# Four small edits in a two-layer transformer trunk: operand places for the first matmuls, and the order and pieces of the last stage

## The chip, the cores and the metric

The kernel runs on one core of one Trainium2 chip. The metric is the device time of one execution in microseconds (us); the times shown are the median of three runs. One execution was also recorded by the hardware profiler, and its trace is what all row times below come from. Five engines work side by side, each through its own list of instructions in order: TensorE (PE, with the weight loads as a row PEld), VectorE (DVE), ScalarE (ACT), GpSimd (POOL) and SyncE (SP), which here issues the large transfers. SBUF is the memory on the chip that the engines read and write; PSUM is the memory that receives the matmul results.

## The reference

Two decoder layers over 512 tokens of width 1024, float32. Cut to what the change touches:

```python
def reference(x, p, positions, ...):
    cos, sin = _rope_tables(positions)
    for i in range(2):
        h = _rms_norm(x, mix_norm[i])
        if i == 0: x = x + _attn_conv_mixer(h, cos, sin, hy_w_in[0], ...)   # q, k, v, cb, cc, cx = split(h @ w_in)
        else:      x = x + _gla_mixer(h, gla_w_in[0], ...)
        x = x + _conv_ffn(_rms_norm(x, ffn_norm[i]), ...)
        x = x + _per_layer_embedding(x, p[i], ple_norm[i], ple_w_gate[i], ple_w_proj[i])
    return x

def _per_layer_embedding(x, p_i, norm, w_gate, w_proj):
    gate = jax.nn.sigmoid(_rms_norm(x, norm) @ w_gate)      # (512 x 1024) @ (1024 x 1024)
    return gate * (p_i @ w_proj)                            # (512 x 256) @ (256 x 1024)
```

The change touches the first matmuls of layer 0 (keys and values, `h @ w_in[:, 512:768]`) and the last stage of layer 1, the per-layer embedding that ends the program.

## The kernel before, in words

**Precision.** A float32 product is made of three matmuls in the type fp32r. Each operand is split into a high part (an ACT copy that rounds) and a low part (a DVE subtraction of the high part from the operand); then high x high, high x low and low x high are summed in PSUM. `mm3` (L162 to L164) does this for most products, `add` in the last stage (L1369 to L1371) for its blocks. So every weight block costs one ACT copy and one DVE subtraction before TensorE may use it.

**Places of split weights.** `wide(tag, at)` gives a tile of 128 partitions by 1088 elements, of which 1024 are used from element `at` on. There are two tags, `wh` for high and `wl` for low parts, with three tiles each, reused in turn. `cut` (L126) is the usual splitter of weights and uses `at` = 0 for both; `cut_blocks` (L811), used in the feed-forward stages (matmuls L872 to L874), uses 16 for `wh` and 48 for `wl`, that is 64 and 192 bytes.

**The start.** In `mixer0`, the input is loaded in four column groups, turned by TensorE (L469), scaled and split, and at once multiplied with the key and value columns of `w_in` (256 columns). Here the activations are the stationary operand of the matmul and the split weights, from `weight(c)`, are the moving one: 8 features of 128 rows, 4 token tiles and 3 matmuls, 96 matmuls of 256 columns in all. The first 12 are at L457 to L460, the rest come through `mm3`. The order on PE, DVE and ACT is the written one here (`manual_schedule`). The query matmuls (512 columns) follow.

**The last stage.** `ple1` (L1323) computes the gate product with a block scheme of Strassen's kind: seven block products instead of eight, with the names `e1`, `s1`, `s2`, `s3`, `s4`, `o2`, `o1` for the activation forms, in this order. Their weights are blocks of 512 x 512: the plain ones `b11`, `b22`, `b21` and differences of them, made in place by `minus` (L1358, two DVE instructions of 128x1024 each, called halves below). `chunk` (L1341) splits half a block: one ACT copy (L1348) and one DVE subtraction (L1349) of 128x1024; its results go to `wh`/`wl` tiles or to tiles called `four`, by a counter, three and three in turn. The products accumulate in four PSUM banks, `X[0]`, `X[1]`, `Q[0]`, `Q[1]`; ACT copies some of the partial sums out (`ka`, `kd`, `kb`; `kd` is made by `keep`, L1401) and DVE adds them later (`summed`, L1407). `back` turns 128 tokens of the residual `x` to token order (TensorE L1377, ACT copy L1381). `proj` multiplies the per-layer input with a half of `w_proj` that `chunk` has split (`wj`): per token tile six matmuls of 512 columns, L162 to L164, into a PSUM bank `pa`. `finish` ends an output tile: ACT sigmoid (L1413), DVE product with the projection (L1414), DVE sum with `x` (L1415), and a transfer to DRAM issued by SP (L1416). All of PE, DVE and ACT follow the written order in this part.

Around the first edit the written order is: `load_p` (the split of the per-layer input, L109/L110), product `s1`, `minus(b12, b22, b12)` (both halves), `kd = keep(Q)`, `wt3 = chunks(b12)` (two splits), `wj = chunk(...)`, four steps of `s2`, two `back`, the other four steps of `s2`, the copies `kb` of `X`, two `proj`, the splits `w22` of `b22`, `minus(b11, b21, b11)`, the first split `wt4[0]`, then product `s3` with `wt3`. A "step" is one j and one i: three matmuls of 512 columns.

At the very end the last product `o1` is done for token tile 0 (512 columns, `Y[0]`) and then for token tile 1 in three pieces of columns: 256 into half of `Q[1]`, then 128 and 128 into two parts of `X[0]`; each piece is finished by itself while the next is multiplied.

Of the kernel before, what the change touches and what calls it, by code (L numbers as in the profile page):

```python
# [56 lines left out]
class Kernel:  # L57
# [65 lines left out]
        t = self.wp.tile([P, 2048], F32, tag="raw", name=self.nm("raw"), bufs=2)  # L123
        return t[:, : na * nb].rearrange("p (a b) -> p a b", b=nb)

    def cut(self, rv, by):  # L126

        nc = self.nc
        na, nb = rv.shape[1:]
        parts = []  # L130
        n = 2 if na * nb > 1024 else 1
        for k in range(n):
            if by == "b":
                a, b = na, nb // n
                v = rv[:, :, k * b : (k + 1) * b]
            else:
                a, b = na // n, nb
                v = rv[:, k * a : (k + 1) * a, :]
            h, l = self.wide("wh"), self.wide("wl")
            hv = h[:, : a * b].rearrange("p (a b) -> p a b", b=b)  # L140
            lv = l[:, : a * b].rearrange("p (a b) -> p a b", b=b)
            nc.scalar.activation(hv, v, AF.Copy)  # L142
            nc.vector.tensor_tensor(lv, v, hv.bitcast(F32), ALU.subtract)  # L143
            parts.append((hv, lv))

        def get(i, c0, c1):
            if by == "b":
                b = nb // n
                k = c0 // b
                h, l = parts[k]  # L150
                return h[:, i, c0 - k * b : c1 - k * b], l[:, i, c0 - k * b : c1 - k * b]
            a = na // n
            h, l = parts[i // a]
            return h[:, i % a, c0:c1], l[:, i % a, c0:c1]

        return get
# [265 lines left out]
    def mixer0(self):  # L422
        nc, a, tc = self.nc, self.a, self.tc
        with tc.tile_pool(name="m0", bufs=1) as mp:
# [3 lines left out]
            kvr = self.raw(ND, 256)  # L428
# [14 lines left out]
            wkv = []  # L443
# [28 lines left out]
                return pss  # L472

            def weight(c):
                wkv.append(self.cut(kvr[:, 2 * c : 2 * c + 2, :], "a"))

            def operand(m, ps):
                hl = self.pair(self.fp, "a0", "a1")
# [38 lines left out]
            h = HD // 2  # L517
# [339 lines left out]
    def seven(self, od, ws, xg, forms, keep=True):  # L857
# [6 lines left out]
        W, V = self.pa(), self.pa()[:, :H]  # L864
        X, Y = self.ps(), self.ps()
        plain, t13, t2 = ws

        def product(out, w, c, x, first=False):
            kw = dict(skip_group_check=True)
            for j in range(ND // 2):  # L870
                (wh, wl), (xh, xl) = w(j, c), x(j)
                mm(out, wh, xh, start=first and j == 0, stop=False, **kw)  # L872
                mm(out, wh, xl, start=False, stop=False, **kw)  # L873
                mm(out, wl, xh, start=False, stop=j == ND // 2 - 1, **kw)  # L874

        def tokens(u, half):
            c = slice(half * H, (half + 1) * H)
            return lambda j: (xg[2 * j + u][0][:, c], xg[2 * j + u][1][:, c])
# [4 lines left out]
        nc.scalar.copy(X[:, left], W[:, left])  # L883
        nc.scalar.copy(Y[:, left], W[:, left])
        yield
# [5 lines left out]
        product(X[:, left], plain, 1, tokens(1, 0))  # L891
        product(Y[:, left], t2, 0, s2)
        nc.scalar.copy(X[:, right], Y[:, left])  # L893
        yield
        last = self.cut_blocks(od)
        product(X[:, right], t13, 1, s3)
        nc.scalar.copy(Y[:, right], X[:, right])
        yield
        product(Y[:, left], last, 1, s4)
        product(X[:, right], last, 0, tokens(1, 1))  # L900
# [422 lines left out]
    def ple1(self, fp):  # L1323
# [3 lines left out]
        nc, a, tc = self.nc, self.a, self.tc  # L1327
# [4 lines left out]
        H, J = D // 2, ND // 2  # L1332

        def block(u, c, own):
            raw = self.raw(J, H) if own else self.four(fp, F32)
            nc.sync.dma_start(raw, wg[u, :, :, c * H : (c + 1) * H])
            return raw
# [3 lines left out]
        def chunk(src):  # L1341
            if count[0] % 6 < 3:
                h, l = (self.wide(g).rearrange("p (a b) -> p a b", b=H) for g in ("wh", "wl"))
            else:
                four = self.four(fp)
                h, l = four[:, :2], four[:, 2:]
            count[0] += 1
            nc.scalar.activation(h, src, AF.Copy)  # L1348
            nc.vector.tensor_tensor(l, src, h.bitcast(F32), ALU.subtract)  # L1349
            return h, l  # L1350

        def chunks(raw):
            return [chunk(raw[:, 2 * q : 2 * q + 2, :]) for q in range(2)]

        def minus(out, x, y):
            for q in range(2):
                c = slice(2 * q, 2 * q + 2)
                nc.vector.tensor_tensor(out[:, c, :], x[:, c, :], y[:, c, :], ALU.subtract)  # L1358

# [28 lines left out]
        def proj(t, w):  # L1388
            pj = self.pa()
            for k in range(2):  # L1390
                self.mm3(pj, sl(pT[k], t), (w[0][:, k, :], w[1][:, k, :]), start=k == 0, stop=k == 1)
            return pj
# [27 lines left out]
        b12 = block(0, 1, True)  # L1420
        pin = self.p_halves(1)
        b22 = block(1, 1, False)
        wj_raw = self.four(fp, F32)
# [6 lines left out]
        X, Q = [[self.ps() for _ in range(2)] for _ in range(2)]  # L1430
        both = (0, H)
        with tc.manual_schedule(engines={ET.PE, ET.DVE, ET.Activation}):
            add(X, "e1", w11, first=True)
            wt1.append(chunk(b11[:, 2:, :]))
            minus(b11, b22, b11)
            steps = [(j, i, both, Q[i]) for j in range(J) for i in range(2)]
            add(None, "s1", wt1, first=True, order=steps[:2])

            self.end_norm()
            ka = [self.sp.tile([P, S], F32, tag="acc", name=self.nm("keep"), bufs=1), self.sq()]  # L1440
            for k, x in zip(ka, X):
                nc.scalar.copy(k, x)
            wt2 = chunks(b11)
            pT = self.load_p(1, fp, pin)
            add(None, "s1", wt1, order=steps[2:])
            minus(b12, b22, b12)
            kd = keep(Q, "R")
            wt3 = chunks(b12)
            wj = chunk(wj_raw[:, 2:, :])
            steps = [(j, i, both, X[i]) for j in range(J) for i in range(2)]  # L1450
            add(None, "s2", wt2, order=steps[:4])
            xs = [back(1, t) for t in (2, 3)]
            add(None, "s2", wt2, order=steps[4:])
            kb = [self.sq(), result()]
            for k, x in zip(kb, X):
                nc.scalar.copy(k, x)
            pjs = [proj(t, wj) for t in (2, 3)]
            w22 = chunks(b22)
            minus(b11, b21, b11)
            wt4 = [chunk(b11[:, :2, :])]  # L1460
            nc.scalar.activation(self.few(NT, "rlo"), self.r, AF.Sigmoid)
            add(X, "s3", wt3)
            ss = [summed(X[t], kd[t]) for t in (0, 1)]
            for t in (0, 1):
                finish(1, t + 2, ss[t], xs[t], pjs[t], ss[t])
            steps = [(j, i, both, Q[i]) for j in range(J) for i in range(2)]
            add(None, "s4", w22, order=steps[:6])
            xs = [back(1, t) for t in (0, 1)]
            pjs = [proj(t, wj) for t in (0, 1)]
            wt4.append(chunk(b11[:, 2:, :]))  # L1470
            wj = chunk(wj_raw[:, :2, :])
            add(None, "s4", w22, order=steps[6:])
            ss = [summed(Q[t], kb[t]) for t in (0, 1)]

            halves = ((0, H // 2), (H // 2, 3 * H // 4), (3 * H // 4, H))
            Y = [Q[0], Q[1][:, : H // 2], X[0][:, : H // 4], X[0][:, H // 4 : H // 2]]
            for t in (0, 1):
                finish(1, t, ss[t], xs[t], pjs[t], ss[t])
            nc.scalar.copy(Y[0], ka[0])
            nc.scalar.copy(Y[1], ka[1][:, : H // 2])  # L1480
            steps = [(j, i, both, X[i]) for j in range(J) for i in range(2)]
            add(None, "o2", wt4, order=steps[:6])
            xs = [back(0, t) for t in (2, 3)]
            pjs = [proj(t, wj) for t in (2, 3)]
            w21 = chunks(b21)
            add(None, "o2", wt4, order=steps[6:])
            for t in (0, 1):
                finish(0, t + 2, X[t], xs[t], pjs[t])
                if t == 0:
                    nc.scalar.copy(X[0][:, : H // 2], ka[1][:, H // 2 :])  # L1490
            add(None, "o1", w21, order=[(j, 0, both, Y[0]) for j in range(J)])
            xs = [back(0, t) for t in (0, 1)]
            pjs = [proj(t, wj) for t in (0, 1)]
            finish(0, 0, Y[0], xs[0], pjs[0])
            for y, c in zip(Y[1:], halves):
                add(None, "o1", w21, order=[(j, 1, c, y) for j in range(J)])
                finish(0, 1, y, xs[1], pjs[1], None, *c)
# [471 lines left out]
```

## Time and profile before

| | us |
|---|---|
| median of 3 runs | 1209.83 (1209.56 to 1209.96) |
| the profiled execution's own time | 1209.6 |
| its span on the core | 1207.8 |
| PE busy in the span | 1199.9 |
| DVE busy | 968.9 |
| ACT busy | 665.2 |

The views used are: the page (busy time and the chain of work that ended last), the table of waits of one engine, the timeline of one engine (start in us, duration in us, engine, line, operation, output from inputs, shape, count; in brackets the idle time before it and what ended it) and the list of transfers. Rows of the timeline that follow each other with the same line, tiles and shape are merged, with their count at the end. Matmuls are pipelined: the duration of one (0.39 us at 512 columns) is longer than the distance from its start to the next start (0.23 us), so lengths of PE work are read from starts.

### The profile page before, as it was taken

Reading aid. Unit: us, or ns where it says so; the run is one execution under the profiler, and the core shown is the slowest. Engines: PE = TensorE matmul, PEld = TensorE weight load, DVE = VectorE, ACT = ScalarE, POOL = GpSimd, SP = SyncE. Lnnn points to the kernel's source line nnn. Section 1 sums busy time; section 2 is a strip of 40 time slices with the busy share of each in tenths; the row PEclk is TensorE's granted clock in tenths of the full one; section 3 lists DMA queues with packets and bytes.
Section 4 is the critical chain, followed back from the end, with each engine's and each line's share of the span. In section 5 each row is a group of like instructions: output and inputs, shape, how many; then the busy total and the mean of one; then the engine's idle time right before and its main releaser. Section 6 shows DMA issues by size and latency. Waiting matters only on the chain.

```text
span 1207.8 us, 17724 instructions
## 1 busy us (share of the span) xinstructions
PE 1199.9 (99%) x7025; PEld 1038.0 (86%) x7025; DVE 968.9 (80%) x1529; ACT 665.2 (55%) x1082; POOL 43.8 (4%) x64
## 2 busy tenths in 40 slices
PE   9999999999999999999999999999999999999998
PEld 8877788999898888888988988889998899888877
DVE  6886687899998987746679876678999898978595
ACT  7466455656555644534563555555565555645364
POOL 2600000000000000000100000000000000000000
PEclk9999999999999999999999999999999999999999
DMA  7321322423233333232322222322242423323501
GB/s 221 95 83 47 95 71 70 140 70 115 96 107 103 102 126 96 96 104 79 113 93 70 72 69 71 105 74 102 73 138 70 140 70 132 122 88 107 199 1 70
DMA packets 111271, 117.61 MB, mean 97 GB/s; under 512 B 2856, under 2 KB 106466, under 8 KB 111188
## 3 DMA queue, kind: packets, MB, share of 16 engines
q1 hardware_dynamic: 109824, 115.35, 29.3%
q8 instruction: 55, 0.90, 0.3%
q0 software_dynamic: 560, 0.42, 0.3%
q10 hardware_dynamic: 804, 0.70, 0.2%
q14 instruction: 28, 0.23, 0.1%
HBM read 114.37 MB, written 2.10 MB: 96 GB/s over the span
## 4 chain that ended last, share of the span: by engine, by line
PE 85%; DVE 9%; ACT 2%; issue 1%; DMA 1%; POOL 1%; ACTq 0%; DVEq 0%; POOLq 0%
PE ps L162 12%; PE ps L163 12%; PE ps L164 12%; PE pa L163 6%; PE pa L162 6%; PE pa L164 6%; PE ps L872 5%; PE ps L874 5%; PE ps L873 5%; PE pa L872 2%; PE pa L874 2%; PE pa L873 2%; DVE wl L143 2%; PE ps L1369 1%; PE ps L1371 1%
## 5 line engine op out<-in xcount | busy, mean ns | idle before, releaser
L142 ACT ACTIVATE wh<-raw 128x1024 fp32r<-128x1024 f32 (+4 forms) x154 | 152.4, 991 | 153.8 <-PE ps L163 109.4
L143 DVE TENSOR_TENSOR wl<-raw,wh 128x1024 fp32r<-128x1024 f32 (+4 forms) x154 | 175.8, 1142 | 49.6 <-ACT wh L142 49.1
L819 ACT ACTIVATE wh<-raw 128x1024 fp32r<-128x1024 f32 x78 | 82.8, 1062 | 119.0 <-DVE raw L844 65.6
L932 DVE SCALAR_TENSOR_TENSOR zt<-z,vfa,zt 128x510 f32<-128x510 f32 (+1 forms) x176 | 130.8, 745 | 11.7 <-ACT zt L930 11.2
L820 DVE TENSOR_TENSOR wl<-raw,wh 128x1024 fp32r<-128x1024 f32 x78 | 95.3, 1222 | 20.9 <-ACT wh L819 20.9
L930 ACT ACTIVATE zt<-z,vfb 128x512 f32<-128x512 f32 x88 | 71.0, 809 | 29.0 <-DVE four L983 12.8
L162 PE MATMUL ps<-b,wh 128*128 128x512 f32 x192 | 76.8, 400 | 0.0
L163 PE MATMUL ps<-b,wh 128*128 128x512 f32 x192 | 75.1, 391 | 0.0
L164 PE MATMUL ps<-b,wl 128*128 128x512 f32 x192 | 75.0, 391 | 0.0
L163 PE MATMUL pa<-b,wh 128*128 128x512 f32 x176 | 69.0, 392 | 0.0
L163 PE MATMUL pa<-a,wh 128*128 128x512 f32 x176 | 69.0, 392 | 0.0
L162 PE MATMUL pa<-a,wh 128*128 128x512 f32 x176 | 69.0, 392 | 0.0
L162 PE MATMUL pa<-b,wh 128*128 128x512 f32 x176 | 69.0, 392 | 0.0
L164 PE MATMUL pa<-a,wl 128*128 128x512 f32 x176 | 68.4, 389 | 0.0
L164 PE MATMUL pa<-b,wl 128*128 128x512 f32 x176 | 68.4, 389 | 0.0
L872 PE MATMUL ps<-four,wh 128*128 128x256 f32 x232 | 65.1, 281 | 0.5 <-ACT ps L893 0.5
L874 PE MATMUL ps<-four,wl 128*128 128x256 f32 x232 | 64.4, 277 | 0.0
L873 PE MATMUL ps<-four,wh 128*128 128x256 f32 x232 | 64.2, 277 | 0.0
L162 PE MATMUL ps<-a,wh 128*128 128x512 f32 x160 | 63.0, 394 | 0.0
L163 PE MATMUL ps<-a,wh 128*128 128x512 f32 x160 | 62.6, 392 | 0.0
L164 PE MATMUL ps<-a,wl 128*128 128x512 f32 x160 | 62.5, 391 | 0.0
L162 PE MATMUL ps<-uh,wh 128*128 128x512 f32 x128 | 50.3, 393 | 0.0
(475 smaller groups left out, 3498.5 us busy)
## 6 DMA issues: line engine op xcount, KB each, us to landing
raw<-in_ffn_w_up_dram SPq DMA_DIRECT2D x44, 1024.0 KB, 5.0
raw<-in_ffn_w_down_dram SPq DMA_DIRECT2D x13, 1024.0 KB, 4.7
raw<-in_hy_w_in_dram SPq DMA_DIRECT2D x8, 1024.0 KB, 5.2
raw<-in_gla_w_in_dram SPq DMA_DIRECT2D x8, 1024.0 KB, 5.3
raw<-in_ffn_w_down_dram SPq DMA_DIRECT2D x8, 768.0 KB, 4.1
raw<-in_ple_w_gate_dram SPq DMA_DIRECT2D x6, 1024.0 KB, 4.8
raw<-in_hy_w_out_dram SPq DMA_DIRECT2D x16, 256.0 KB, 3.9
raw<-in_gla_w_out_dram SPq DMA_DIRECT2D x4, 1024.0 KB, 4.7
```

The costliest lines, as they stand in the source:

```text
L142: nc.scalar.activation(hv, v, AF.Copy)
L143: nc.vector.tensor_tensor(lv, v, hv.bitcast(F32), ALU.subtract)
L162: mm(out, lh, rh, start=start, stop=False, **kw)
L163: mm(out, lh, rl, start=False, stop=False, **kw)
L164: mm(out, ll, rh, start=False, stop=stop, **kw)
L819: nc.scalar.activation(h, src, AF.Copy)
L820: nc.vector.tensor_tensor(l, src, h.bitcast(F32), ALU.subtract)
L872: mm(out, wh, xh, start=first and j == 0, stop=False, **kw)
L873: mm(out, wh, xl, start=False, stop=False, **kw)
L874: mm(out, wl, xh, start=False, stop=j == ND // 2 - 1, **kw)
L930: nc.scalar.activation(y, z, AF.Identity, scale=w2[:, f : f + 1], bias=bb[:, f : f + 1])
L932: nc.vector.scalar_tensor_tensor(out=y[:, tap:], in0=z[:, : S - tap], scalar=w[:, f : f + 1], in1=y[:, tap:], op0=ALU.mult, op1=ALU.add,)
```

## The change

1. **Places of the key and value weights.** `cut` takes a pair `at`; `weight(c)` in `mixer0` passes (48, 16), so the high parts of the key and value weights start 192 bytes and the low parts 64 bytes into their tiles. Every other caller keeps 0.
2. **The projection's split first.** `wj = chunk(wj_raw[:, 2:, :])` moves ahead of `kd = keep(Q, "R")` and of the splits of `b12`.
3. **The second half of a difference later.** `minus(b12, b22, b12)` is done in two calls: the first half where it was, the second half after the split of the first half, `wt3[0]`. The split of the second half, `wt3[1]`, moves from there to behind the copies `kb` of the sums `X` (on ACT, behind them in order; on DVE it stays the next subtraction after the second half).
4. **The last 512 columns in two pieces.** `halves` has two entries, 256 and 256 columns; the second piece goes into half of `X[0]`.

With the edits 2 and 3 the tiles of the splits change too: the counter hands the projection the place in turn that the first half of `b12` had, and so on by one; all are of the kind `wh`/`wl` as before. On DVE the order in the stage is now: difference half one, `wj`, `wt3[0]`, difference half two, `wt3[1]`, `w22`. On ACT: `wj`, the two copies `kd`, `wt3[0]`, the two `back` copies, the two copies `kb`, `wt3[1]`, `w22`. With edit 4, PE has 12 matmuls fewer, DVE two instructions, ACT and SP one each. No instruction changes its place on POOL, and no other transfer moves.

```diff
-    def cut(self, rv, by):
+    def cut(self, rv, by, at=(0, 0)):
...
-            h, l = self.wide("wh"), self.wide("wl")
+            h, l = self.wide("wh", at[0]), self.wide("wl", at[1])
...
-                wkv.append(self.cut(kvr[:, 2 * c : 2 * c + 2, :], "a"))
+                wkv.append(self.cut(kvr[:, 2 * c : 2 * c + 2, :], "a", (48, 16)))
...
-        def minus(out, x, y):
-            for q in range(2):
+        def minus(out, x, y, parts=(0, 1)):
+            for q in parts:
...
-            minus(b12, b22, b12)
+            minus(b12, b22, b12, (0,))
+            wj = chunk(wj_raw[:, 2:, :])
             kd = keep(Q, "R")
-            wt3 = chunks(b12)
-            wj = chunk(wj_raw[:, 2:, :])
+            wt3 = [chunk(b12[:, :2, :])]
+            minus(b12, b22, b12, (1,))
...
             pjs = [proj(t, wj) for t in (2, 3)]
+            wt3.append(chunk(b12[:, 2:, :]))
             w22 = chunks(b22)
...
-            halves = ((0, H // 2), (H // 2, 3 * H // 4), (3 * H // 4, H))
-            Y = [Q[0], Q[1][:, : H // 2], X[0][:, : H // 4], X[0][:, H // 4 : H // 2]]
+            halves = ((0, H // 2), (H // 2, H))
+            Y = [Q[0], Q[1][:, : H // 2], X[0][:, : H // 2]]
```

## The prediction

> **What bounds the kernel.** I read the page first, then the waits of PE, then the timelines of the first 22 us and the last 60 us.
>
> ```profile
> span 1207.8 us, 17724 instructions
> PE 1199.9 (99%) x7025; PEld 1038.0 (86%) x7025; DVE 968.9 (80%) x1529; ACT 665.2 (55%) x1082; POOL 43.8 (4%) x64
> ```
>
> ```profile
> PE pa L163 <- DVE wl L1349: 0.9, 1, 0.9
> PE pa L653 <- ACT pT L661: 0.5, 1, 0.5
> PE ps L1369 <- ACT so L1413: 0.5, 1, 0.5
> ```
>
> PE is busy 1199.9 of 1207.8 us: matmul work sets the time. Three of its waits stand above (total, times, longest). The first is a projection matmul in the last stage that waits for the low part of its weights, the third is the last 128-column piece. So time can be gained only by shortening PE's work, its few waits, or the tail after its last matmul. The edits aim at one of each kind.
>
> **The change part by part.**
>
> *Edits 2 and 3, the wait of the projection.* PE, then DVE and ACT of the stage:
>
> ```profile
> 1164.87 0.39 PE L1371 MATMUL ps<-four,a 128*128 128x512 f32 x1
> 1165.29 0.50 PE L162 MATMUL pa<-wh,four 128*128 128x512 f32 x1
> 1166.74 0.50 PE L163 MATMUL pa<-wl,four 128*128 128x512 f32 x1 [0.95 <-DVE wl L1349]
> 1167.08 0.39 PE L164 MATMUL pa<-wh,four 128*128 128x512 f32 x1
> ...
> 1172.09 0.39 PE L1369 MATMUL ps<-wh,a 128*128 128x512 f32 x1
> ...
> 1179.69 0.48 PE L162 MATMUL pa<-wh,four 128*128 128x512 f32 x1
> ...
> 1180.23 0.39 PE L164 MATMUL pa<-wh,four 128*128 128x512 f32 x1
> ```
>
> ```profile
> 1159.65 1.28 DVE L110 TENSOR_TENSOR four<-pa,four 128x512 fp32r<-128x512 f32 x2
> 1160.85 2.35 DVE L1358 TENSOR_TENSOR raw<-four,raw 128x1024 f32<-128x1024 f32 x2
> 1163.18 2.37 DVE L1349 TENSOR_TENSOR wl<-raw,wh 128x1024 fp32r<-128x1024 f32 x2
> 1165.47 1.22 DVE L1349 TENSOR_TENSOR wl<-four,wh 128x1024 fp32r<-128x1024 f32 x1
> 1168.16 2.36 DVE L1349 TENSOR_TENSOR four<-four,four 128x1024 fp32r<-128x1024 f32 x2 [1.48 <-ACT four L1348]
> ...
> 1174.33 1.37 DVE L1407 TENSOR_TENSOR so<-ps,keep 128x512 f32<-128x512 f32 x2 [0.26 <-PE ps L1371]
> ```
>
> ```profile
> 1158.61 1.08 ACT L1401 COPY keep<-ps 128x512 f32<-128x512 f32 x2
> 1162.09 2.20 ACT L1348 ACTIVATE wh<-raw 128x1024 fp32r<-128x1024 f32 x2 [2.40 <-DVE raw L1358]
> 1164.20 1.04 ACT L1348 ACTIVATE wh<-four 128x1024 fp32r<-128x1024 f32 x1
> 1165.14 1.05 ACT L1381 COPY zt<-pa 128x512 f32<-128x512 f32 x2
> 1166.08 0.60 ACT L1456 COPY sq<-ps 128x512 f32<-128x512 f32 x1
> ```
>
> From the projection's first to its third matmul PE takes 1167.08 - 1165.29 = 1.79 us here and 1180.23 - 1179.69 = 0.54 us in the next projection, which does not wait: the stall costs 1.25 us (the bracket says 0.95; the rest is the restart). Its cause is order: DVE makes two difference halves and two other low parts first and reaches `wl<-four` only at 1165.47.
>
> With the new order DVE does, from 1160.85 on and one every 1.15 us (2.35 for two): difference half one, the projection's low part (1162.0 to 1163.2), the low part of `wt3[0]` (1163.2), half two (1164.3 to 1165.5). The projection's operand is there 2.1 us before PE asks for it at 1165.29; its ACT copy goes in at 1158.61, in front of the `kd` copies. These come 1 us later, and nothing is behind them: their first reader is the sum at 1174.33, and `wt3[0]`'s copy needs difference half one, so it stays at 1162.1. So 1.25 us go; the lower bound is the bracket's 0.95.
>
> What is late next? `wt3[1]`. Its ACT copy is now behind the copies of `X`, which wait for the last matmul of `s2` (1164.87 + 0.39 = 1165.3): with 0.5 us for that copy it starts at 1165.8 and ends at 1166.9, the DVE part (1.23) at 1168.1. PE wants it in the third quarter of `s3`, at 1172.09 now and 1.25 earlier then: 1170.84, so 2.7 us are left. `w22` follows on DVE at 1168.1, as before (1168.16), and the difference of `b11` behind it and the sums at 1174.33 stay where they are or come 0.5 us earlier; no queue gets longer. I add nothing for a new wait; the range keeps up to 0.3 us for one.
>
> The moved steps issue no transfers. One more place: the turn of the `wh`/`wl` tiles has moved by one, so the second half of `wt4` might get the tile that the two later projections still read. By the rows they end then at 1181.4 (1.25 before 1182.7); copy and subtraction (1.06 + 1.23) would make it ready at 1183.8, and PE asks for it at 1185.3 (1186.59 now):
>
> ```profile
> 1182.28 0.39 PE L164 MATMUL pa<-wh,four 128*128 128x512 f32 x1
> ...
> 1186.59 0.39 PE L1369 MATMUL ps<-wh,a 128*128 128x512 f32 x1
> ```
>
> Even then 1.5 us are left.
>
> *Edit 4, the last pieces.*
>
> ```profile
> 1199.29 0.28 PE L1369 MATMUL ps<-wh,b 128*128 128x256 f32 x1
> ...
> 1200.72 0.22 PE L1369 MATMUL ps<-wh,b 128*128 128x128 f32 x1
> ...
> 1202.68 0.33 PE L1369 MATMUL ps<-wh,b 128*128 128x128 f32 x1 [0.51 <-ACT so L1413]
> ```
>
> ```profile
> 1202.33 0.33 SPq L1416 DMA_DIRECT2D out_dram<-so  x1
> ```
>
> ```profile
> 1205.31 0.33 SPq L1416 DMA_DIRECT2D out_dram<-so  x1
> ```
>
> ```profile
> out_dram<-so SPq DMA_DIRECT2D x1, 128.0 KB, 1.8
> out_dram<-so SPq DMA_DIRECT2D x2, 64.0 KB, 1.5
> ```
>
> The 256-column piece takes 1200.72 - 1199.29 = 1.43 us for its 12 matmuls; the 128-column piece behind it takes 1202.68 - 1200.72 = 1.96 us until its successor may start, because that one, in the same bank, waits for the sigmoid that reads it. From its first matmul to the issue of its transfer the 256-column piece takes 1202.33 - 1199.29 = 3.04 us. The new last piece is the same work, starts at 1200.72, and so issues at 1203.76 instead of 1205.31: 1.55 us. ACT and DVE are clear of the piece before it: that one is done at its issue, 1202.33, and the new piece's last matmul starts only at 1200.72 + 11 x 0.12 = 1202.04, its sigmoid after its end. The larger transfer lands in 1.8 instead of 1.5 us: the net is 1.25 us. Bounds: 1.0 and 1.55.
>
> *Edit 1, the places.* Two steady runs of 256-column matmuls, first and last rows: 41 distances of the key/value matmuls, 23 in the feed-forward.
>
> ```profile
> 16.21 0.28 PE L162 MATMUL pa<-wh,a 128*128 128x256 f32 x1
> ...
> 21.13 0.28 PE L164 MATMUL pa<-wh,a 128*128 128x256 f32 x1
> ```
>
> ```profile
> 189.57 0.28 PE L872 MATMUL ps<-a,wh 128*128 128x256 f32 x1
> ...
> 192.17 0.28 PE L874 MATMUL ps<-four,sq 128*128 128x256 f32 x1
> ```
>
> That is 4.92 / 41 = 0.120 us against 2.60 / 23 = 0.113 us for the same shape. The faster run has its stationary operands 64 and 192 bytes into their tiles, the slower has everything at 0. Edit 1 makes the same distances between moving and stationary operand, with the roles exchanged. If the distance is what matters, 96 matmuls gain 0.007 us each, at most 0.65 us. The first 12 are written in another order, and transposes interrupt the start three times, so I take 0.5. The other end: no row shows a steady run above 0.120, so a loss isn't seen; I allow the half of the gain, 0.3 us, since roles and not only distances may count. ACT and DVE splits cost the same at either place (128x1024: 1058 and 1062 ns on ACT, in the rows of L142 and L819).
>
> ```profile
> L142 ACT ACTIVATE wh<-raw 128x1024 fp32r<-128x1024 f32 x119 | 125.6, 1058 | 116.4 <-PE ps L163 80.3 <-PE ps L873 16.8 <-PE ps L164 7.6
> L819 ACT ACTIVATE wh<-raw 128x1024 fp32r<-128x1024 f32 x78 | 82.8, 1062 | 119.0 <-DVE raw L844 65.6 <-PE ps L873 16.3 <-PE ps L163 14.2
> ```
>
> Does a gain at 20 us reach the end? PE waits at 88 us for `pT` (0.5 us, above), the end of a long ACT and DVE chain. That chain starts when PE hands over the first query:
>
> ```profile
> 41.56 0.69 ACT L570 ACTIVATE q<-ps,rtok 128x512 f32<-128x512 f32 x1 [2.34 <-PE ps L164]
> ```
>
> So it moves with PE, and no later wait of PE names a transfer. I let all of it through.
>
> The Trainium skill, TensorE: Matmul & The Clock Gate, "Step-by-step: what each phase is for", speaks against this edit: the weight load and the moving operand have separate read ports, and loading the next weights "doesn't steal SBUF read bandwidth from the running matmul". By that rule edit 1 gives 0 and the sum is 2.5 us; by the two rows above, 3.0. The rows differ in pitch with the same clock and shape, so I go by them, but they differ in roles too, and the rule keeps a chance below.
>
> *Sum.* 1.25 + 1.25 + 0.5 = 3.0 us. The profiled execution of 1209.6 becomes 1206.6; the median shown is 0.2 above it, so I predict 1206.8.
>
> **The rivals.**
>
> *The places do nothing* (the 0.120 comes from the roles of the operands or from what precedes, not from the distance). For it: the 512-column runs have their operands at 0 too, and no pair of rows in this trace differs in place alone. Time 1209.8 - 2.5 = 1207.3. This is the rival that the quoted rule stands behind; it is just at the limit of what counts as a difference.
>
> *Part of the last stage's gain returns as a new wait*, or the key/value matmuls get slower by the 0.3 us allowed. Against it stand 2.7 and 1.5 us of slack. Time about 1208.0.
>
> *Slower: the third quarter of `s3` becomes the wait.* Place: PE at L1370 with `wt3[1]`, whose copy now stands behind the copies of `X` on ACT. Price: every us past 1170.84 is a us of PE time. If it were ready at 1173.3 the 2.5 us of the stage would be gone; for a slowdown of 0.2% it must come 2.4 us later still or more, about 1176, that is 8 us after my 1168.1, for instance if the ACT copy waited for `s3`'s first half or for the sums. Time then 1212. Nothing before it in the queue waits that long in the rows.
>
> **How the numbers follow.** A measurement here tells about 0.2%, 2.4 us, from no change: the limit is 1207.4. Chances: forecast 0.62 (1206.2 to 1207.3), places do nothing 0.20, partial return 0.13, slower 0.05. The forecast is faster nearly always (0.59); the second rival, at 1207.3, a little more often than not (0.12); the third stays within 0.2%. So 0.71 faster, 0.24 same, 0.05 slower. Range: the best ends, 1.25 + 1.55 + 0.65 = 3.45, give 1206.4, with 0.2 for the scatter of the runs 1206.2; at the top, 0.95 + 1.0 and nothing from edit 1 give 1207.9.
>
> **What would show it.** Edit 1: distances of 0.113 to 0.115 in the key/value run, and the first query matmul 0.5 us earlier than 21.49; at 0.120 it failed. Edits 2 and 3: the wait of L163 for L1349 gone from PE's list, `s3`'s third quarter without a bracket. Edit 4: two 256-column runs of 1.43 us each, no bracket between them, 3.0 us from the last run's first matmul to the last issue. The forecast is wrong if a new wait of PE over 0.5 us appears between 1165 and 1196, or if the start's gain is taken back by a longer wait at 88 us.
>
> ```profile
> 21.49 0.50 PE L162 MATMUL ps<-wh,a 128*128 128x512 f32 x1
> ```

## The result, and the profile after

The changed kernel takes 1206.60 us, the median of nine runs (1206.16 to 1207.34), against 1209.87 us for the kernel before on the same chip (nine runs, 1209.14 to 1210.16). The ratio is 0.9975 with a 95% interval of 0.9966 to 0.9983: 3.3 us faster, a quarter of a percent, and the interval leaves "no change" outside. 1206.8 was predicted. The profiled execution took 1206.43 us, of it 1204.7 in the span.

Page of the changed kernel: the span, and the busy time of each engine.

```profile
span 1204.7 us, 17692 instructions
PE 1197.7 (99%) x7013; PEld 1036.9 (86%) x7013; DVE 968.3 (80%) x1527; ACT 665.3 (55%) x1081; POOL 43.8 (4%) x64
```

The span is 3.1 us shorter and PE's busy time 2.2 us (1199.9 to 1197.7). Its waits (total, times, longest, in us), as far as the list goes:

```profile
PE pa L198 <- DVE mhalf L186: 1.3, 1, 1.3
PE ps L872 <- ACT ps L893: 0.5, 2, 0.3
PE pa L653 <- ACT pT L661: 0.5, 1, 0.5
PE ps L162 <- DVE kT L1558: 0.2, 1, 0.2
```

The two waits of the last stage, L163 for `wl` and L1369 for `so`, are gone and no new wait of that stage has come in. Timeline of PE after, in the last stage and in the key/value run (start, duration):

```profile
1161.15 1.04 PE L1377 MATMUL pa<-cf,xT 128*128 128x128 f32 x8
...
1164.53 0.39 PE L1371 MATMUL ps<-four,a 128*128 128x512 f32 x1
1164.76 0.39 PE L162 MATMUL pa<-wh,four 128*128 128x512 f32 x1
1164.99 0.39 PE L163 MATMUL pa<-wl,four 128*128 128x512 f32 x1
1165.21 0.39 PE L164 MATMUL pa<-wh,four 128*128 128x512 f32 x1
...
1197.39 0.28 PE L1369 MATMUL ps<-wh,b 128*128 128x256 f32 x1
...
1198.83 0.28 PE L1369 MATMUL ps<-wh,b 128*128 128x256 f32 x1
...
1200.15 0.28 PE L1371 MATMUL ps<-four,a 128*128 128x256 f32 x1
```

```profile
16.26 0.28 PE L162 MATMUL pa<-wh,a 128*128 128x256 f32 x1
...
21.08 0.28 PE L164 MATMUL pa<-wh,a 128*128 128x256 f32 x1
21.45 0.50 PE L162 MATMUL ps<-wh,a 128*128 128x512 f32 x1
```

The projection now runs at 0.23 us per matmul from the last matmul of `s2` on, without a gap. The last two pieces start 1198.83 - 1197.39 = 1.44 us apart, with no bracket (a bracket at the end of a row is the idle time before it). The key/value run, however, takes 4.82 / 41 = 0.1176 us per matmul: hardly less than the 0.120 before, and far from the 0.113 that was predicted for it.

DVE and ACT after, in the same stage, show the new order:

```profile
1160.50 1.21 DVE L1358 TENSOR_TENSOR raw<-four,raw 128x1024 f32<-128x1024 f32 x1
1161.63 1.21 DVE L1349 TENSOR_TENSOR wl<-four,wh 128x1024 fp32r<-128x1024 f32 x1
1162.84 1.23 DVE L1349 TENSOR_TENSOR wl<-raw,wh 128x1024 fp32r<-128x1024 f32 x1
1163.98 1.22 DVE L1358 TENSOR_TENSOR raw<-four,raw 128x1024 f32<-128x1024 f32 x1
1166.54 1.23 DVE L1349 TENSOR_TENSOR wl<-raw,wh 128x1024 fp32r<-128x1024 f32 x1 [1.34 <-ACT wh L1348]
```

```profile
1158.27 1.06 ACT L1348 ACTIVATE wh<-four 128x1024 fp32r<-128x1024 f32 x1
...
1165.44 1.06 ACT L1348 ACTIVATE wh<-raw 128x1024 fp32r<-128x1024 f32 x1
```

The projection's low part is done at 1161.63 + 1.21 = 1162.8, and its first reader, L163, starts at 1164.99. The second split of `b12` ends on DVE at 1167.8; the third quarter of `s3` follows some 2.6 us later, without a bracket. The last transfer is issued by SP here:

```profile
1201.88 0.33 SPq L1416 DMA_DIRECT2D out_dram<-so  x1
```

From the last piece's first matmul to this it is 1201.88 - 1198.83 = 3.05 us.

**A measure for the last stage.** The time from PE's first matmul to the last stage differs by up to 1 us between recordings, also where no edit lies in it. So I measure the stage by itself, from its first turned tile (the row of L1377 with eight matmuls), to the start of the last matmul, to the issue of the last transfer, and to the end, which is the start of the last record in the trace. In the kernel before the first and the last of its PE rows are:

```profile
1161.49 1.04 PE L1377 MATMUL pa<-cf,xT 128*128 128x128 f32 x8
...
1203.96 0.28 PE L1371 MATMUL ps<-four,a 128*128 128x128 f32 x1
```

| from the first L1377 group of the stage, us | last matmul | last issue | end |
|---|---|---|---|
| before | 42.47 | 43.82 | 46.24 |
| after | 38.99 | 40.72 | 43.45 |
| gain | 3.48 | 3.10 | 2.79 |

The first column gains most because the tail behind the last matmul is longer with a last piece of 256 columns: 1.73 us to the issue against 1.35, and 2.73 us from there to the end against 2.42. The third column is what the time sees: 2.79 us of the 3.27 us between the medians arise here.

### The profile page after: what moved, and what is told of

Read it like the earlier page. It is cut to its first block, busy times and chain, and to the rows that moved or that the text cites. A ratio compares the mean times of both kernels' runs of the same rounds, so it can differ in the third digit from the quotient of the medians.

```text
span 1204.7 us, 17692 instructions
## 1 busy us (share of the span) xinstructions
PE 1197.7 (99%) x7013; PEld 1036.9 (86%) x7013; DVE 968.3 (80%) x1527; ACT 665.3 (55%) x1081; POOL 43.8 (4%) x64
## 4 chain that ended last, share of the span: by engine, by line
PE 87%; DVE 8%; ACT 2%; issue 1%; POOL 1%; DMA 0%; ACTq 0%; DVEq 0%; POOLq 0%
PE ps L162 12%; PE ps L163 12%; PE ps L164 12%; PE pa L163 7%; PE pa L162 7%; PE pa L164 7%; PE ps L872 5%; PE ps L874 5%; PE ps L873 5%; PE pa L872 2%; PE pa L874 2%; PE pa L873 2%; DVE wl L143 2%; PE ps L1371 1%; PE ps L1369 1%
## 5 line engine op out<-in xcount | busy, mean ns | idle before, releaser
L163 PE MATMUL ps<-b,wh 128*128 128x512 f32 x192 | 75.1, 391 | 0.0
L163 PE MATMUL pa<-b,wh 128*128 128x512 f32 x176 | 69.0, 392 | 0.0
L163 PE MATMUL pa<-a,wh 128*128 128x512 f32 x176 | 69.0, 392 | 0.0
L163 PE MATMUL ps<-a,wh 128*128 128x512 f32 x160 | 62.6, 392 | 0.0
```

Of the source, the lines that this page charges most:

```text
L163: mm(out, lh, rl, start=False, stop=False, **kw)
```

## The experiments

### Each part alone

Places alone is edit 1 in the kernel before, order alone is edits 2 and 3, pieces alone is edit 4. Their diffs are those parts of the change's diff:

```diff
-                wkv.append(self.cut(kvr[:, 2 * c : 2 * c + 2, :], "a"))
+                wkv.append(self.cut(kvr[:, 2 * c : 2 * c + 2, :], "a", (48, 16)))
```

> The kernel before with edit 1 alone (key/value weights 192 and 64 bytes into their tiles). Theory (the place matters): the steady distance of the key/value matmuls falls from 0.120 to the 0.1175 us that the trace of the changed kernel shows (7.03 us for 59 distances with one start of 0.20, against 7.15 before), so PE reaches the query 0.2 to 0.3 us earlier relative to the first of these matmuls; time 1209.5 to 1209.7, a difference that the timing can hardly tell. Rival (separate read ports, the place is nothing): distance 0.120 as before, time as before, and the 0.35 us by which PE was early at 1160 us in the changed kernel are jitter of the start.

```diff
-            minus(b12, b22, b12)
-            kd = keep(Q, "R")
-            wt3 = chunks(b12)
+            minus(b12, b22, b12, (0,))
             wj = chunk(wj_raw[:, 2:, :])
+            kd = keep(Q, "R")
+            wt3 = [chunk(b12[:, :2, :])]
+            minus(b12, b22, b12, (1,))
...
+            wt3.append(chunk(b12[:, 2:, :]))
             w22 = chunks(b22)
```

> The kernel before with edits 2 and 3 alone (projection's split first, second half of the difference later). Theory: PE's wait of 0.95 us at the projection is gone with its restart and with a smaller wait before its first matmul that the prediction left out; 1.25 us by the prediction's sum, 1.5 us by the changed kernel's rows; the time falls by that, to 1208.3 to 1208.7, and the last two waits (three pieces) stay. Rival (part returns as a new wait at the third quarter of s3): a bracket at L1370 there and a gain under 1.0 us.

```diff
-            halves = ((0, H // 2), (H // 2, 3 * H // 4), (3 * H // 4, H))
-            Y = [Q[0], Q[1][:, : H // 2], X[0][:, : H // 4], X[0][:, H // 4 : H // 2]]
+            halves = ((0, H // 2), (H // 2, H))
+            Y = [Q[0], Q[1][:, : H // 2], X[0][:, : H // 2]]
```

> The kernel before with edit 4 alone (two pieces of 256). Theory: the last transfer is issued 1.55 us earlier and lands 0.3 us later after its issue, net 1.25 us: 1208.6. Rival (the shorter tail of a 128-column piece is worth more than its matmuls): no gain, 1209.9 or slower. The gains of the three edits alone should add up to the 3.1 us of all of them, since they lie at three places of one PE chain.

The fourth run is the changed kernel with the two places of the key/value weights exchanged:

```diff
-                wkv.append(self.cut(kvr[:, 2 * c : 2 * c + 2, :], "a", (48, 16)))
+                wkv.append(self.cut(kvr[:, 2 * c : 2 * c + 2, :], "a", (16, 48)))
```

> The changed kernel with the two places of edit 1 exchanged (high parts 64, low parts 192 bytes on), which turns the sign of the distance between the moving and the stationary operand and leaves its size modulo 256 bytes as another pair of 64 and 192. Theory (only that the high and low parts lie 128 bytes apart matters): the same 0.1175 us, time as the changed kernel, 1206.6. Other theory (the signed distance counts): another distance between 0.113 and 0.122 us, up to 0.4 us either way. Rival (no effect of places): 0.120 as in the kernel before.

| | median, us | ratio to before, 95% interval | stage to its end, against before, us |
|---|---|---|---|
| places alone | 1209.23 | 0.9999 (0.9990 to 1.0008) | +0.01 |
| order alone | 1208.31 | 0.9991 (0.9983 to 1.0000) | -1.56 |
| pieces alone | 1208.38 | 0.9990 (0.9981 to 0.9999) | -1.21 |
| all, places exchanged | 1206.54 | 0.9975 (0.9965 to 0.9984) | -2.80 |
| kernel before, same chip | 1209.52 | | |

The waits of PE with order alone keep the one of the last piece, those with pieces alone keep the one of the projection. A row of each list:

```profile
PE ps L1369 <- ACT so L1413: 0.5, 1, 0.5
```

```profile
PE pa L163 <- DVE wl L1349: 1.0, 1, 1.0
```

So of the two waits of the last stage, order and pieces each take away the one they were matched with, and not the other. By the stage's length order and pieces add up: 1.56 + 1.21 = 2.77 us against 2.79 for all. By the medians alone the parts could not be told apart that finely, since each interval is about as wide as the effect.

The places give nothing that the time shows. The steady distance is 0.1178 us with either assignment of the two places, against 0.120: 96 matmuls gain 96 x 0.0022 = 0.2 us. That is less than the start scatters: from PE's first matmul to the stage's first L1377 group the recordings of before, after and the four parts are between 1159.8 and 1160.4 us long, with no order by edit: before is 1160.2, places alone and after are 1159.8, and pieces alone, which changes nothing there, is 1160.4.

### What the order is worth, and how much slack it leaves

In the first run the split of `b12`'s second half is put two steps further back, behind the splits of `b22` and the difference of `b11`. In the second, edit 3 is undone and of the two only edit 2 is left (the projection's split ahead of the whole difference).

```diff
-            wt3.append(chunk(b12[:, 2:, :]))
             w22 = chunks(b22)
             minus(b11, b21, b11)
+            wt3.append(chunk(b12[:, 2:, :]))
```

> The changed kernel with the split of the difference's second half moved two steps further back, behind the splits of b22 and the difference of b11. This measures the slack that the prediction gave to the third quarter of s3 (2.7 us) and the price past it (a us of PE for each us). In the changed kernel that subtraction starts on DVE at 1166.5 and ends at 1167.8; four DVE instructions of 128x1024 in front of it (2.35 for two) put its end at about 1172.5, and PE asks for it at about 1170.3: theory: a new wait of about 2.2 us at L1370 of s3, the end 2 us later than the changed kernel's. Rival (something else sets s3's third quarter, or the slack is larger than read): no bracket there, time unchanged.

```diff
-            minus(b12, b22, b12, (0,))
             wj = chunk(wj_raw[:, 2:, :])
+            minus(b12, b22, b12)
             kd = keep(Q, "R")
-            wt3 = [chunk(b12[:, :2, :])]
-            minus(b12, b22, b12, (1,))
+            wt3 = chunks(b12)
...
-            wt3.append(chunk(b12[:, 2:, :]))
```

> The changed kernel with edit 3 undone: the projection's split goes first, but both halves of the difference and both of its splits follow it together, as they did before the change. Theory (the wait came from the place of the projection's split alone): PE has no wait in the stage, and from the first transposes of the stage to the last matmul it takes the same 38.99 us as in the changed kernel; edit 3 is worth nothing. Rival (the second half in front keeps the first split of the difference or the copies of X late): a bracket at the projection or at s3, up to 1.2 us.

Timeline of PE with the third quarter late:

```profile
1160.79 1.04 PE L1377 MATMUL pa<-cf,xT 128*128 128x128 f32 x8
...
1169.84 0.39 PE L1369 MATMUL ps<-four,a 128*128 128x512 f32 x1
1172.00 0.50 PE L1370 MATMUL ps<-four,a 128*128 128x512 f32 x1 [1.77 <-DVE four L1349]
1172.33 0.39 PE L1371 MATMUL ps<-four,a 128*128 128x512 f32 x1
...
1201.85 0.28 PE L1371 MATMUL ps<-four,a 128*128 128x256 f32 x1
```

The wait comes back at the place the "slower" rival named, L1370 with `wt3[1]`: a bracket of 1.77 us, and the stage ends 45.52 - 43.45 = 2.07 us later than after. The one run took 1208.14 us. About 0.3 us of the price is again not in the bracket. The starts show where it is: from L1369 to L1370 it is 1172.00 - 1169.84 = 2.16 us instead of 0.23, which is 1.93 lost. The bracket begins only where the row of L1369 ends, 0.39 us after its start, so it leaves out 0.39 - 0.23 = 0.16 of that. The next distance, 0.33 us, is another 0.10 too long.

Timelines of PE and of DVE with the projection's split first and nothing else moved:

```profile
1160.88 1.04 PE L1377 MATMUL pa<-cf,xT 128*128 128x128 f32 x8
...
1199.87 0.28 PE L1371 MATMUL ps<-four,a 128*128 128x256 f32 x1
```

```profile
1160.23 1.21 DVE L1349 TENSOR_TENSOR wl<-four,wh 128x1024 fp32r<-128x1024 f32 x1
1161.36 2.35 DVE L1358 TENSOR_TENSOR raw<-four,raw 128x1024 f32<-128x1024 f32 x2
1163.70 2.36 DVE L1349 TENSOR_TENSOR wl<-raw,wh 128x1024 fp32r<-128x1024 f32 x2
```

From the first L1377 group to the last matmul it is 38.99 us, as in the changed kernel; the one run took 1206.19 us. So edit 3 is worth nothing here: edit 2 without it takes the wait away.

### The pieces of the last 512 columns

One piece of 512 columns, and three pieces as in the kernel before, but with the third in a bank of its own (`X[1]`):

```diff
-            halves = ((0, H // 2), (H // 2, H))
-            Y = [Q[0], Q[1][:, : H // 2], X[0][:, : H // 2]]
+            halves = ((0, H),)
+            Y = [Q[0], Q[1]]
...
-            nc.scalar.copy(Y[1], ka[1][:, : H // 2])
+            nc.scalar.copy(Y[1], ka[1])
...
```

> The changed kernel with the last 512 columns in one piece. From the rows of the changed kernel: 12 matmuls at 0.2266 us are 2.72 us against 2.87 for 24 at 0.12, so the last matmul ends 0.05 us earlier; the sigmoid, product and sum of 512 columns (0.72 + 0.72 + 0.69) then take 2.16 us to the issue against 1.42, and the larger transfer lands 0.2 us later after its issue (2.0 against 1.8): the issue comes 0.6 us and the end 0.8 us later. Rival (a piece costs more than it hides, so fewer are better still): the end earlier than in the changed kernel.

```diff
-            halves = ((0, H // 2), (H // 2, H))
-            Y = [Q[0], Q[1][:, : H // 2], X[0][:, : H // 2]]
+            halves = ((0, H // 2), (H // 2, 3 * H // 4), (3 * H // 4, H))
+            Y = [Q[0], Q[1][:, : H // 2], X[0][:, : H // 4], X[1][:, : H // 4]]
...
-                if t == 0:
-                    nc.scalar.copy(X[0][:, : H // 2], ka[1][:, H // 2 :])
+                nc.scalar.copy(X[t][:, : H // 4], ka[1][:, (2 + t) * H // 4 : (3 + t) * H // 4])
```

> The changed kernel with the three pieces of the kernel before (256, 128, 128), but each in a bank of its own, so that none waits for the sigmoid of another. It parts edit 4's gain into the wait and the matmuls. Theory (0.113 us for a 128-column matmul as the rows of before show, and no wait): last matmul 0.6 us before that of the kernel before and 1.25 us after that of the changed kernel; the issue 0.88 us and the end (the smaller transfer lands 0.3 us sooner) 0.58 us after the changed kernel's. Rival (the wait was all of it): the end with the changed kernel's or before it. Other rival (the wait is not the bank's): the bracket at the last piece stays.

| last 512 columns | time, us | last issue against after, us | end against after, us |
|---|---|---|---|
| 256 + 256 (after) | 1206.60 | 0 | 0 |
| 512 | 1207.69 (one run) | +0.60 | +0.83 |
| 256 + 128 + 128, three banks | 1206.47 (one run) | +0.82 | +0.52 |
| 256 + 128 + 128, two banks (order alone) | 1208.31 | +1.55 | +1.24 |

The times of single runs don't decide here, since the start scatters by as much as the effect; the stage's lengths do. Timeline of PE with three banks:

```profile
1160.66 1.04 PE L1377 MATMUL pa<-cf,xT 128*128 128x128 f32 x8
...
1198.33 0.22 PE L1369 MATMUL ps<-wh,b 128*128 128x128 f32 x1
...
1199.62 0.27 PE L1369 MATMUL ps<-wh,b 128*128 128x128 f32 x1
...
1200.85 0.28 PE L1371 MATMUL ps<-four,a 128*128 128x128 f32 x1
```

With a bank of its own, the third piece starts 1199.62 - 1198.33 = 1.29 us after the second, not 1.96 as before, and has no bracket. So the wait comes from sharing the bank, as the prediction read it. It is a wait for a semaphore of ACT that the program sets on the third piece's first matmul when the two pieces share a bank; what the chip would do without that semaphore no run shows. Of edit 4's 1.24 us to the end 1.24 - 0.52 = 0.72 us are this wait. The other 0.52 us is what 256 + 256 gains on 256 + 128 + 128 without a wait: the last matmul comes 1.20 us earlier (1200.15 - 1198.83 = 1.32 us behind the start of the second piece, not 1200.85 - 1198.33 = 2.52), less a tail that is 0.38 us longer to the issue and 0.30 us longer from there to the end. With 512 columns in one piece the last matmul comes another 0.26 us earlier, and the tail to the issue is 0.86 us longer: ACT and DVE then work on all of them after it.

### Places, for all weights

The first run gives every weight that `cut` splits the places that the feed-forward has, 64 bytes for high and 192 for low parts; the key/value weights keep theirs. The second takes a pair of places per chunk of the key/value weights. The third hands eight pairs in turn to all weights of `cut`; the numbers in the pairs are elements of 4 bytes.

```diff
-            h, l = self.wide("wh", at[0]), self.wide("wl", at[1])
+            h, l = self.wide("wh", at[0] or 16), self.wide("wl", at[1] or 48)
```

> The changed kernel, in which every other split of weights by cut also lies 64 (high) and 192 (low) bytes into its tiles; the key/value weights as in the changed kernel. Theory (the place matters wherever the weight load and the moving operand read side by side): the 512-column matmuls, 0.2266 us apart in steady runs, come closer, and 1 ns over some 4800 of them is 5 us; a gain of up to 30 us if they lose as much as the 256-column ones. Rival (at 512 columns the weight load has time to spare and the place is nothing): distance 0.2266 as before, time 1206 to 1207. Second rival: it gets worse for 336 and 368 columns, under 2 us.

```diff
-                wkv.append(self.cut(kvr[:, 2 * c : 2 * c + 2, :], "a", (48, 16)))
+                wkv.append(self.cut(kvr[:, 2 * c : 2 * c + 2, :], "a", ((0, 32), (0, 16), (16, 0), (32, 0))[c]))
```

> The changed kernel with a pair of places of its own for each of the four key/value weight chunks, 24 matmuls each: high and low parts (0, 128), (0, 64), (64, 0) and (128, 0) bytes on. Theory (only that high and low parts lie 128 bytes apart counts): 0.1177 us in the first and the last chunk, 0.120 in the two between. Theory of the distance to the stationary operand (at 64 and 192 bytes it is free, at 0 it collides): matmuls with the operand at 0 lose 0.007 us, the others nothing, so all four chunks lie between 0.113 and 0.120. Rival: 0.120 in all. The time of the whole moves by under 0.3 us.

```diff
+        self.turn = 0
...
+        if at == (0, 0):
+            at = ((0, 0), (16, 48), (48, 16), (0, 32), (0, 16), (16, 0), (32, 32), (8, 40))[self.turn % 8]
+            self.turn += 1
```

> The changed kernel in which cut takes eight pairs of places in turn, one pair a call (in bytes: 0/0, 64/192, 192/64, 0/128, 0/64, 64/0, 128/128, 32/160), to read from one trace what each does to matmuls of 512, 368 and 336 columns. Theory (places matter at 512 columns too): runs of calls differ, with distances between 0.220 and 0.2333 us, some below the 0.2266 of now. Rival: 0.2266 to 0.227 in all of them, and the time 1206 to 1207.

Places for all weights, expected to gain, make the kernel slower: 1216.48 us, ratio 1.0062 (1.0045 to 1.0079) to the kernel before. Places in turn took 1216.25 us and the four pairs 1206.37 us, one run each. The page with places for all:

```profile
span 1214.8 us, 17692 instructions
PE 1208.8 (100%) x7013; PEld 1038.3 (85%) x7013; DVE 969.0 (80%) x1527; ACT 666.3 (55%) x1081; POOL 43.8 (4%) x64
```

The instructions are the same and PE keeps their order, yet PE is busy 11.1 us longer than after, DVE and ACT 0.7 and 1.0. The list of PE's waits holds no new one. The groups of PE by line and shape (count, busy us and mean ns of one), first after and then with places for all, show which matmuls got longer:

```profile
L163 PE MATMUL pa<-a,wh 128*128 128x512 f32 x176 | 69.0, 392 | 0.0
...
L164 PE MATMUL pa<-a,wl 128*128 128x512 f32 x176 | 68.4, 389 | 0.0
```

```profile
L164 PE MATMUL pa<-a,wl 128*128 128x512 f32 x176 | 69.8, 396 | 0.0
...
L163 PE MATMUL pa<-a,wh 128*128 128x512 f32 x176 | 69.0, 392 | 0.0
```

The rows of those with the low part stationary, 192 bytes into its tile, got 7 ns longer each; the rows of the same tiles with the high part, 64 bytes in, did not. The ends of these rows are modelled, so the starts count more: over all such matmuls, the mean distance from the start of one to the start of the next went from 227.3 to 235.4 ns with the low part stationary, and from 228.3 to 229.9 with the high part. The rows below are a steady run of 512-column matmuls in each kernel, after and with places for all.

```profile
125.37 0.40 PE L162 MATMUL ps<-a,wh 128*128 128x512 f32 x1
...
130.82 0.39 PE L162 MATMUL ps<-a,wh 128*128 128x512 f32 x1
```

```profile
126.44 0.40 PE L162 MATMUL ps<-a,wh 128*128 128x512 f32 x1
...
130.84 0.39 PE L163 MATMUL ps<-a,wh 128*128 128x512 f32 x1
```

That is 5.45 / 24 = 0.2271 us after, and 4.40 / 19 = 0.2316 us with places for all. Summed row by row, the 3072 matmuls of 512 columns with these weights stationary take 10.3 us more from start to start than in the changed kernel (the expectation had put the number of such matmuls at some 4800), and everything else on PE together 0.2 us less. That is the whole difference of the two spans, 1214.8 - 1204.7.

In places in turn, the mean distance of the 512-column matmuls with the weights stationary, worked out from the starts of the rows, is 228.2 ns at the pair (0, 0) and between 231.2 and 233.1 at the seven others. With the weights moving only two of the pairs occur at 512 columns, in the two halves of the query weights: 227.1 ns at (0, 0) and 230.6 at 64 and 192 bytes. At 256 columns the key/value run shows the opposite sign and less of it: by the four pairs of the second run the mean distances per feature, in order of the features and without the longer distances at the starts, are 117.1 and 117.9, 117.9 and 117.9, 117.9 and 118.9, 119.4 and 119.9 ns. The last pair, 128 bytes for the high and 0 for the low part, is near the 120 of before, the others are near the 117.8 of edit 1. So it is not only 128 bytes between the parts that counts, since of the two such pairs one gains and the other hardly does; and no pair brings 0.113.

So place does change the pace of matmuls. At 256 columns moving weights gain 1 to 2 ns from some pairs; at 512 columns zero for both is the best of the eight tried. The weights' places change both where PE reads and where ACT and DVE write. Places in turn separates the two, since ACT and DVE write ahead at another pair than the one that PE reads: the matmuls during which no split weights are written at all are 228.1 ns apart at (0, 0) and 231.1 to 233.1 at the other pairs, much as the rest are. So what counts is the place that PE reads from. Why it counts isn't shown.

## Why the prediction was right, and where its terms were off

The predicted time, 1206.8 us, is 0.2 above the median, and the forecast "faster" holds. Its three terms were not equally good. One was 0.3 us low and one 0.3 us high; that their sum, 2.97 us by the parts' own measures, comes so near to the 3.0 predicted is luck. The other 0.3 us of the 3.27 between the medians lie in no term; the start scatters by more.

**Projection's wait, 1.25 us predicted: 1.56 measured.** Mechanism and place were right: the wait is gone and DVE has the new order. The size was low. The prediction compared PE's first three projection matmuls (1.79 us) with the next projection (0.54 us). Without the wait they take 1165.21 - 1164.76 = 0.45 us, and PE no longer pauses ahead of the first: 1165.29 - 1164.87 = 0.42 us before, 1164.76 - 1164.53 = 0.23 after. 1.34 + 0.19 = 1.53 us. Edit 3, with its second half and the third quarter, adds nothing to this: without it the stage has the same length.

**Slack of 2.7 us for `wt3[1]`.** Right: no bracket after. Put two steps later, the price was a bracket of 1.77 and a stage 2.07 us longer. "Every us past 1170.84 is a us of PE time" needs some 0.3 us added for what the bracket leaves out. The rival "slower" had its place right; its wait did not appear. The 1.5 us of slack for the second half of `wt4` weren't tested by themselves; no wait of that stage appeared.

**Last pieces, 1.25 us predicted: 1.21 measured.** Two runs of 1.44 us, no bracket, 3.05 us from first matmul to issue: all three signs are there. The prediction did not divide it; three banks do: of the 1.24 us measured there, 0.72 us is the shared bank's wait and 0.52 us the wider matmuls net of their tail.

**Places, 0.5 us predicted: 0.2 by the distances.** This is the failed step. (At its own prices the upper bound is 96 x 0.007 = 0.67 us, not 0.65.) The distance became 0.1178, not 0.113 to 0.115; the first query matmul came 21.49 - 21.45 = 0.04 us earlier in the timeline, not 0.5. The prediction took the feed-forward's distance to depend on the places because its weights are placed apart; with the same places the key/value run does not reach it. What else sets the 0.113 stays open: the roles of the operands, for instance, are different there, and no run changed them. The rival "the places do nothing" comes nearer on this term. Its total, 1207.3, is further from the median than the forecast, because the projection's term was low and 0.3 us lie in no term.

**That rival's rule.** The Trainium skill, TensorE: Matmul & The Clock Gate, "Step-by-step: what each phase is for", has separate read ports, so that a weight load takes no bandwidth from the running matmul. For the key/value run at 256 columns it is right within 2 ns. As a ground for "places never matter" it fails here: at 512 columns the same instructions in the same order take 3 to 5 ns longer each, in the mean, with the weights at other places, and the whole kernel 10 us. The place that counts is the one that PE reads. What the ports have to do with it no run shows.

**The start's gain passing through the wait at 88 us.** Not decided: a gain of 0.2 us is below the scatter of the start, and the wait for `pT` stands at 0.5 us as before.

## What to carry to other kernels

Measure a late stage from an event inside it, not from the start of the program: here the length of the same stage repeats to 0.04 us (43.45 to 43.49 in five kernels), where the way to it scatters by up to 1 us, and experiments could be told apart that the medians could not. Where a matmul waits for a split that stands behind others in order, move that split alone ahead, read the slack of what it pushes back, and price a wait by starts and not by its bracket. The distance of matmuls in other roles was no price for a tile's place here: the price needs a run in the same role and at the same column count.

## What the runs showed of the hardware

The pace of 512-column matmuls depends on where the split weights that PE reads start in their SBUF tiles: by 3 to 5 ns of 228 for stationary weights, where the start of the tile is the best of the eight pairs tried, and by 3.5 ns of 227 for moving weights, at the one other pair that occurs. At 256 columns some other starts gain 1 to 2 ns of 120. Matmuls into a part of a PSUM bank waited, by a semaphore of the program, while ACT read another part: a bank for each piece was worth 0.72 us. Where PE waits, it loses more than the bracket states: 2.07 us against 1.77 in `s3`'s third quarter, and 1.56 against 0.95 at the projection.
